# Repricing loads, scans and transposes in the builder of a hybrid encoder kernel, and moving some transfers back in SyncE's order

## The chip, the cores and the metric

The kernel runs on one core of a Trainium2 chip. The metric is the device time of one launch in microseconds (us), lower is better; several runs of a kernel are made and their median is taken. One more execution was recorded by the hardware profiler, and all rows below come from it. The engines are TensorE (PE, with its weight loads as PEld), VectorE (DVE), ScalarE (ACT), GpSimd (POOL) and SyncE (SP), which computes nothing here and issues most of the DMAs. An SPq row is such an issue.

## The reference, cut to what matters

Two layers of a streaming encoder act on 2048 new prompt frames and on 8 running streams of 16 frames, 1024 columns wide. Each layer is one input projection, three mixers beside each other, one output projection and a LayerNorm:

```python
proj = x @ lp["w_in"]
a_sh, a_z, b_q, b_k, b_v, b_f, b_z, c_qkv, c_b, c_a, c_z = split_cols(proj, SPLIT)
o_a, rwkv_last, rwkv_s = rwkv_mix(a_sh, a_z, rwkv_prev, rwkv_s0, lp)
...
o_b = fox_prompt(q, k, v, logf)       # prompt; fox_cached(...) for the streams
...
o_c, conv_last, gdn_s = gdn_mix(c_qkv, c_b, c_a, c_z, gdn_conv_prev, gdn_s0, lp)
h = jnp.concatenate([o_a, o_b, o_c], axis=-1) @ lp["w_out"]
x_new = layer_norm(ALPHA * x + h, lp["ln_g"], lp["ln_b"])
```

`rwkv_mix` and `gdn_mix` are delta-rule recurrences (4 heads of 64 each), which the kernel does in chunks of 64 frames with a small triangular inverse per chunk. `fox_prompt` is causal softmax attention with 8 heads and a cumulative forget term; `fox_cached` is the same against a cache of 1024 rows per stream.

## The kernel before

**Stages.** For each layer the input projection is done in thirds of 640, 768 and 768 columns of tokens (`proj`, line 536). Weights come in blocks of 128 columns (`load_w`, line 427): SyncE loads `wr` (512 KB, two buffers), ACT makes the rounded half `wh`, POOL (or DVE for the v blocks) the rest `wl`. The first time a block is used, `wl` is also stored to the DRAM tensor `wd`; later thirds load it from there. Each product is three matmuls (`pm`, or `pv` for the v blocks). The recurrences (`rwkv_*`, `gdn_*`, `inverse`, `both_chain`, `post`; the "rg" tasks) are woven between the projection's matmuls in sub-blocks of 256 tokens. Then comes attention over the prompt (`fox_prompt`, line 1740), with the streams' attention (`fox_sample`, line 1793) woven in, and at last the output projection (`out_proj`, line 1932).

**What sets the order.** Nothing is measured while the kernel is built. The builder keeps a clock of its own, `Model` (line 105): each instruction gets a start time from when its operands are done, when its output tile is free, and when its engine has room (`place`, line 142), and a cost from `Model.cost` (line 154). The time becomes the instruction's scheduling priority, and for SyncE it also fixes the order: `Eng.order` (line 252) chains each DMA behind the one with the next smaller time, from the recurrences' start to the end of attention in each layer (`pin`). On the chip an engine's queue, SyncE's too, goes in that order and an instruction that waits holds those behind it. TensorE's order comes from the same clock: `Task.wake` and `drive` (line 466) put a task's matmuls between projection matmuls when the clock says that their operands are ready. A wrong price does not change what is waited for on the chip, only who stands in front of whom.

The prices that matter here: a DVE instruction costs 0.065 us plus elements per partition over 960 (1920 for some); a SyncE DMA occupies the queue for max(0.5, bytes / 3.6e5) us and lands 2.0 us later (lines 182 to 186). A read from a DRAM tensor does not wait in the clock for the write to it.

**Places that the change touches.** `load_w` stores `wd`. In `proj` the k and q blocks are split into `khi` and `klo`, which are stored to `ks` and `qs`; their tiles share the tag `z4` (three buffers) with `xin`, the tiles that bring in the tokens of the next third (`load_x`, line 511), and with the log-forget tiles of `logf` (line 677), stored to `ck`, `sm`, `lx` and the outputs. `gate` (line 1512) loads `z` for a recurrence's output. `inverse` and `inverse2` use DVE's square transposes (`N<-NB`, `TT<-Wi`, `T<-TT`); `rwkv_a`, `logf` and `fox_sample` use `tensor_tensor_scan`. `fox_sample` loads cache pieces `kc` and `vc` of 1 MB each, writes its cumulative sums to the DRAM tensor `SC` and reads them back as `S`. `open_o` (line 1918) loads the output weights `wor`, 8 times 512 KB, when `fox_sample` is done. `open_fx` (line 1569) opens attention's tiles once the projection's are free:

```python
self.QA = self.QA0 + [pool.tile([128, 512], F32R, name=f"QA{j}") for j in range(2, 6)]
self.KA = self.KA0 + [pool.tile([128, 1024], F32R, name=f"KA{j}") for j in range(2, 6)]
self.fx_fill(nc.gpsimd, self.KA[2:], self.QA[2:])
self.fx_qa(l, 0, 1)
```

`fx_fill` (line 1550) writes constants into rows 64 and up of these tiles on POOL; `fx_qa` (line 1620) loads rows 0 to 63 of two QA tiles. The attention's first matmuls are `mx` (the row maxima, `fx_max`, line 1634) and `st` (the scores, `fx_exp`, line 1668). Every instruction but a matmul has the helper's line 246 in the profile; matmuls have 224, transposes on TensorE 227.

Of the kernel before, what the change touches and what calls it, by code (L numbers as in the profile page):

```python
# [14 lines left out]
TS = 16  # L15
PAST = 1024
# [88 lines left out]
class Model:  # L105
# [4 lines left out]
    def __init__(self, tc):  # L110
        self.tc, self.t, self.pin = tc, 0.0, 0
        self.done, self.used, self.busy, self.rings, self.by = {}, {}, {}, {}, {}
        self.held = set()

    def tile(self, ap, key, bufs):
# [38 lines left out]
    def cost(self, eng, kind, n, outs, ins):  # L154
        cols = sum(1 for a in ins if numel(a) == 1 and a.shape[0] > 1)
        psum = any(a.space == bass.MemoryType.PSUM for a in ins)
        if eng == "vector":
            fast = kind in ("tensor_scalar", "tensor_copy", "memset") and not psum
            return 0.065 * (1 + cols) + n / (1920.0 if fast else 960.0)
        if eng == "scalar":  # L160
            return (0.05 if psum else 0.095) + 0.09 * cols + n / 1200.0
        if kind == "memset":
            return 0.05 + n / 1220.0
        return 0.05 + 0.27 * cols + n / 440.0

# [100 lines left out]


class NC:
    def __init__(self, nc, model):
        self.tensor = nc.tensor  # L270
        for n in ("vector", "scalar", "gpsimd", "sync"):
            setattr(self, n, Eng(n, getattr(nc, n), model))


# [24 lines left out]
class Trunk:  # L299
# [127 lines left out]
    def load_w(self, pool, key, src, kk, n, eng):  # L427
        nc = self.nc
        raw = pool.tile([128, kk, n], F32, tag="wr", name="wr", bufs=2)
        wh = pool.tile([128, kk, n], F32R, tag="wh", name="wh", bufs=2)  # L430
        wl = pool.tile([128, kk, n], F32R, tag="wl", name="wl", bufs=2)
        for ap, c in src:
            m = ap.shape[1]
            nc.sync.dma_start(raw[:, :, c:c + m], ap.rearrange("(k p) n -> p k n", p=128))
        nc.scalar.copy(wh, raw)
        if key in self.wd:
            nc.sync.dma_start(wl.bitcast(F32), self.wd[key])
        else:
            eng.tensor_tensor(wl, raw, wh.bitcast(F32), op=ALU.subtract)
            self.wd[key] = self.dram.tile([128, kk, n], F32, name="wd_" + "_".join(map(str, key)))  # L440
            nc.sync.dma_start(self.wd[key], wl.bitcast(F32))
        return wh, wl
# [93 lines left out]
    def proj(self, l, ti, groups, nxt=None):  # L536
# [91 lines left out]
        for nm, c0, S, X in (("k", 1664, self.KS[l], self.KX[l]), ("q", 1152, self.QS[l], self.QX[l])):  # L628
            if nm not in groups:
                continue  # L630
            for r in range(0, 512, 128):
# [8 lines left out]
                nc.vector.tensor_tensor(lo[:, ns:n], st[:, ns:n], hi[:, ns:n].bitcast(F32), op=ALU.subtract)  # L640
                nc.sync.dma_start(S[0, r:r + 128, tp], hi[:, ns:n].bitcast(F32))
                nc.sync.dma_start(S[1, r:r + 128, tp], lo[:, ns:n].bitcast(F32))
                if ns:
# [33 lines left out]
    def logf(self, l, ti, fs):  # L677
# [10 lines left out]
        nc.vector.scalar_tensor_tensor(out=lt, in0=f, scalar=0.0, in1=ab, op0=ALU.min, op1=ALU.subtract)  # L688
        nc.sync.dma_start(self.o["fox_logf_p"][l, 0, tp].rearrange("(j p) h -> p j h", p=128), lt[:, ns // 128:])
        if ns:  # L690
            nc.sync.dma_start(self.o["fox_logf_s"][l].rearrange("s t h -> (s t) h"), lt[:, 0])
        nc.vector.tensor_scalar(f, lt, -1.0, None, op0=ALU.mult)
        nc.sync.dma_start(self.SM[l][t0:t0 + n].rearrange("(j p) c -> p j c", p=128), fs[:, :, 8:16])
        yield
# [7 lines left out]
        if ns:  # L702
            nc.sync.dma_start(self.LX[l].rearrange("s h t -> h s t"), fr[0:8, 0:ns].rearrange("h (s t) -> h s t", t=TS))
        cr = pool.tile([8, 768], F32, tag="st", name="cr", bufs=2)
# [5 lines left out]
        self.split(ch[:, ns:n], cl[:, ns:n], cr[:, ns:n], "vector")  # L710
        nc.sync.dma_start(self.CK[l][0, :, tp], ch[:, ns:n].bitcast(F32))
        nc.sync.dma_start(self.CK[l][1, :, tp], cl[:, ns:n].bitcast(F32))

# [577 lines left out]
    def both_chain(self, x):  # L1291
# [66 lines left out]
        if x["t0"] + W == NTOK:  # L1358
            dst = self.o["gdn_wkv_p"][x["l"]].rearrange("s (p h) k v -> s p (h k) v", h=2)
            for p in range(2):  # L1360
                nc.sync.dma_start(dst[0, p], self.Sg[:, p])

# [95 lines left out]
    def gdn_chain(self, x):  # L1458
# [50 lines left out]
        for p in range(2):  # L1509
            nc.sync.dma_start(dst[:, p].rearrange("s k v -> k s v"), SS[:, :, p])  # L1510

    def gate(self, x, r0, y, name):
        nc, W = self.nc, x["W"]
        z = self.rt("z", [128, 2, W])
        nc.sync.dma_start(z, self.PZ[x["l"]][r0:r0 + 256, x["t0"]:x["t0"] + W].rearrange("(q p) t -> p q t", p=128))
# [34 lines left out]
    def fx_fill(self, eng, KA, QA):  # L1550
        for t in QA + KA:
# [17 lines left out]
    def open_fx(self, l):  # L1569
# [223 lines left out]
    def fox_sample(self, l):  # L1793
# [3 lines left out]
        kx = pool.tile([128, 4, 128], F32, name="kx")  # L1797
        nc.sync.dma_start(qx, self.QX[l].rearrange("(c p) t -> p c t", p=128))
        nc.sync.dma_start(kx, self.KX[l].rearrange("(c p) t -> p c t", p=128))
        qbd = pool.tile([128, NS, 4, 32], F32, name="qbd")  # L1800
# [4 lines left out]
        lf = pool.tile([128, NS, 8, 8], F32, tag="vn", name="lf", bufs=2)  # L1805
        nc.sync.dma_start(lf, i["cache_fox_logf"][l].rearrange("s (p j) h -> p s j h", j=8))
        lr = pool.tile([64, PAST + TS], F32, tag="S", name="lr64", bufs=2)
# [5 lines left out]
        def load(s, nm, hf):  # L1813
            if s < NS:
                t = kv[s, nm, hf] = pool.tile([128, 4, 512], F32, tag=nm, name=nm, bufs=4)
                nc.sync.dma_start(t, i["cache_fox_" + nm[0]][l, s, hf * 512:hf * 512 + 512].rearrange("(j p) h d -> p j (h d)", p=128))

# [6 lines left out]
        for j0 in (0, 4):  # L1824
# [3 lines left out]
            nc.scalar.mul(lv[:, j0:j0 + 4], p[0:64].rearrange("p (j t) -> p j t", j=4), -1.0)  # L1828
        nc.sync.dma_start(lr[:, PAST:], self.LX[l].rearrange("s h t -> (s h) t"))
        cr = pool.tile([64, PAST + TS], F32, tag="S", name="cr64", bufs=2)  # L1830
# [78 lines left out]
        z = pool.tile([128, 4, 128], F32, tag="vn", name="sfz", bufs=2)  # L1909
        nc.sync.dma_start(z, self.PZ[l][256:768, 0:SMP].rearrange("(c p) t -> p c t", p=128))  # L1910
# [4 lines left out]
        nc.sync.dma_start(self.OD[l][256:768, 0:SMP].rearrange("(c p) t -> p c t", p=128), oT)  # L1915
        self.close(pool)
# [154 lines left out]
```

## Time and profile before

| | us |
|---|---|
| median of 3 runs | 4135.79 (4131.1 to 4138.03) |
| the profiled execution, its own time | 4139.12 |
| its span in the profile | 4137.2 |
| PE busy, share of the span | 3776.2, 91% |
| DVE, ACT, POOL busy | 2700.3, 1637.1, 1223.7 |
| mean granted TensorE clock | 0.95 |

The span is what the profile covers; the profiled execution's own time lies 1.9 us above it and 3.3 us above the median. PE's busy time counts a matmul as longer when the granted clock is low, so a busy PE is not PE at its peak. Idle time of an engine matters only where PE, the busiest engine, ends up waiting for it. In a timeline row the bracket at the end gives the idle time of the engine before the instruction and what ended it.

### The profile page before, as it was taken

What the parts mean: (1) busy time and instruction counts of PE and PEld (TensorE: products, weight loads), DVE (VectorE), ACT (ScalarE), POOL (GpSimd) and SP (SyncE); (2) the same over time, 40 slices, a digit from 0 to 9 for tenths busy, and PEclk for the clock granted to TensorE, in tenths of its full rate; (3) what the DMA queues carried; (4) which work ended last, traced back from release to release, by engine and by line L of the source; (5) the groups of instructions that cost most, each with busy time, mean ns of one, the idle gap of its engine ahead of it and who ended that gap; (6) DMA issues with size and microseconds to landing.
All of it is one profiled execution on the core that took longest, in us unless ns stands there. A gap on an engine that the chain in (4) does not pass through costs nothing.

```text
span 4137.2 us, 78111 instructions
## 1 busy us (share of the span) xinstructions
PE 3776.2 (91%) x30554; PEld 3107.2 (75%) x30554; DVE 2700.3 (65%) x6029; ACT 1637.1 (40%) x3351; POOL 1223.7 (30%) x1073
## 2 busy tenths in 40 slices
PE   6989998999998799889999898989999888998998
PEld 6988887888887456557888888878888775665577
DVE  6475668677774677774523757577667767777645
ACT  2343434344442344542124434244435424444411
POOL 4311232122212344454222112312122124444522
PEclk9999999999998899999999999999999989999999
DMA  7744545444555677443456445554445555774332
GB/s 262 238 154 129 155 141 173 123 139 127 173 156 138 187 192 195 138 102 111 135 157 192 134 133 151 168 153 127 141 128 186 154 131 164 199 195 124 105 115 102
DMA packets 601754, 633.80 MB, mean 153 GB/s; under 512 B 153625, under 2 KB 457483, under 8 KB 601387
## 3 DMA queue, kind: packets, MB, share of 16 engines
q1 hardware_dynamic: 535228, 543.89, 45.1%
q10 hardware_dynamic: 63406, 76.01, 5.2%
q0 software_dynamic: 2752, 8.92, 0.6%
q8 instruction: 241, 3.95, 0.4%
q14 instruction: 127, 1.03, 0.1%
HBM read 437.59 MB, written 191.10 MB: 152 GB/s over the span
## 4 chain that ended last, share of the span: by engine, by line
PE 54%; DVE 19%; issue 10%; DMA 8%; POOL 4%; ACT 3%; SPq 1%; ACTq 0%; POOLq 0%; DVEq 0%
PE pm L224 21%; PE op L224 6%; PE st L224 5%; PE fo L224 4%; PE mx L224 3%; DVE itmp L246 2%; PE pv L224 2%; DVE Wi L246 2%; PE cr L224 2%; DVE y L246 2%; PE co L224 2%; DMA pc<-pc 2%; DVE xs L246 1%; DVE m L246 1%; PE cg L224 1%
## 5 line engine op out<-in xcount | busy, mean ns | idle before, releaser
L224 PE MATMUL pm<-xh,wh 128*128 128x384 f32 (+1 forms) x2784 | 987.1, 355 | 4.8 <-ACT wh L246 4.8
L224 PE MATMUL pm<-xh,wl 128*128 128x384 f32 (+1 forms) x2784 | 924.5, 332 | 23.4 <-DMA wl<-wd 14.1
L224 PE MATMUL pm<-xl,wh 128*128 128x384 f32 (+1 forms) x2784 | 923.3, 332 | 0.0
L224 PEld LDWEIGHTS pm<-xh,wh 128*128 128x128 f32 x2784 | 533.4, 192 | 43.9 <-issue 17.0
L224 PEld LDWEIGHTS pm<-xh,wl 128*128 128x128 f32 x2784 | 532.6, 191 | 27.1 <-DMA wl<-wd 16.5
L224 PEld LDWEIGHTS pm<-xl,wh 128*128 128x128 f32 x2784 | 534.0, 192 | 10.2 <-issue 9.8
L246 POOL TENSOR_TENSOR acc<-acc,pt 128x512 f32<-128x512 f32 (+2 forms) x336 | 378.3, 1142 | 347.0 <-ACT pt L246 314.0
L246 DVE TENSOR_REDUCE m<-mx 128x1 f32<-128x512 f32 (+3 forms) x640 | 371.4, 605 | 160.4 <-PE mx L224 151.6
L246 ACT ACTIVATE pt<-st 128x512 f32<-128x512 f32 (+3 forms) x640 | 330.9, 533 | 341.8 <-PE st L224 319.7
L246 ACT CAST wh<-wr 128x1024 fp32r<-128x1024 f32 (+1 forms) x198 | 207.3, 1049 | 316.8 <-PE pm L224 237.3
L224 PE MATMUL mx<-KA,QA 66*128 66x512 f32 (+3 forms) x640 | 265.1, 437 | 40.0 <-DMA QA<-qs 26.0
L224 PE MATMUL st<-QB,KB 128*128 128x512 f32 (+3 forms) x640 | 266.7, 417 | 32.1 <-DMA QB<-qs 10.7
L224 PE MATMUL fo<-pt,V 128*64 128x512 f32 (+3 forms) x1280 | 286.8, 570 | 1.1 <-ACT pt L246 1.1
L246 ACT COPY st<-pm 128x384 f32<-128x384 f32 (+1 forms) x348 | 159.2, 457 | 279.7 <-PE pm L224 265.0
L224 PE MATMUL st<-QA,KA 104*128 104x512 f32 (+3 forms) x640 | 244.0, 381 | 0.2
L246 POOL TENSOR_SCALAR SD<-Sr,dl 128x64 f32<-128x64 f32 x128 | 66.9, 537 | 594.5 <-DVE Sr L246 517.9
L224 PEld LDWEIGHTS mx<-KA,QA 66*128 66x128 f32 x640 | 128.8, 206 | 113.3 <-issue 47.0
L224 PE MATMUL op<-woh,oh 128*128 128x512 f32 x544 | 213.0, 392 | 0.7 <-ACT acc L246 0.7
L224 PE MATMUL op<-wol,oh 128*128 128x512 f32 x544 | 212.5, 391 | 0.0
L224 PE MATMUL op<-woh,ol 128*128 128x512 f32 x544 | 212.4, 390 | 0.0
L246 POOL TENSOR_TENSOR wl<-wr,wh 128x1024 fp32r<-128x1024 f32 x58 | 142.1, 2451 | 191.9 <-ACT wh L246 171.6
L246 DVE TENSOR_TENSOR itmp<-N,Wi 128x126 f32<-128x126 f32 (+22 forms) x558 | 178.7, 320 | 15.1
(378 smaller groups left out, 7616.8 us busy)
## 6 DMA issues: line engine op xcount, KB each, us to landing
wr<-in_w_in SPq DMA_DIRECT2D x198, 512.0 KB
wl<-wd SPq DMA_DIRECT2D x116, 512.0 KB
kc<-in_cache_fox_k SPq DMA_DIRECT2D x32, 1024.0 KB
vc<-in_cache_fox_v SPq DMA_DIRECT2D x32, 1024.0 KB
wd<-wl SPq DMA_DIRECT2D x58, 512.0 KB
xin<-xd SPq DMA_DIRECT2D x78, 256.0 KB
y<-xd SPq DMA_DIRECT2D x34, 512.0 KB
ol<-od SPq DMA_DIRECT2D x34, 512.0 KB
```

Source lines behind the costliest of these rows:

```text
L224: self.add(lambda: self.eng.matmul(out, a, b, start=start, stop=stop), out, a, b, cyc, start)
L246: r = f(*a, **b)
```

## The change

The builder's prices: square transposes and scans on DVE cost 0.065 + n/500 (n/960 before); SyncE DMAs occupy the queue at 3.2e5 bytes per us (3.6e5 before) and land 3.0 us later (2.0 before); a read from `SC` waits in the clock for its write. A second handle for SyncE, `nc.lag`, places a DMA 6 us later in the clock than its operands allow. It is the same queue and the same DMA; only its place in the order moves. `open_fx` issues the QA load ahead of the constants and fills two QA tiles ahead of the rest.

```diff
         if eng == "vector":
+            if kind in ("transpose", "tensor_tensor_scan"):
+                return 0.065 + n / 500.0
...
             if a.space == bass.MemoryType.DRAM:
                 dram = True
+                if a.tensor.name.startswith("SC"):
+                    t = max(t, self.done.get(a.tensor.name, 0.0) - self.lag)
...
         if eng == "sync":
             n = max(n * a.shape[0] for a in outs)
-            cost = max(0.5, n * 4 / 3.6e5)
-            end = self.place(eng, t, cost) + 2.0
-            t = end - 2.0 - cost
+            cost = max(0.5, n * 4 / 3.2e5)
+            end = self.place(eng, t + self.lag, cost) + 3.0
+            t = end - 3.0 - cost
...
+class Lag:
+    BY = 6.0
+    def __init__(self, eng, model):
+        self.eng, self.m = eng, model
+    def dma_start(self, *a):
+        self.m.lag = self.BY
+        r = self.eng.dma_start(*a)
+        self.m.lag = 0.0
+        return r
...
-        self.fx_fill(nc.gpsimd, self.KA[2:], self.QA[2:])
         self.fx_qa(l, 0, 1)
+        self.fx_fill(nc.gpsimd, (), self.QA[2:4])
+        self.fx_fill(nc.gpsimd, self.KA[2:], self.QA[4:])
```

These DMAs go from `nc.sync` to `nc.lag`: the stores to `wd` (not those of other tensors in `load_w`), `ks`, `qs`, `ck`, `sm`, `lx`, the log-forget outputs, the `gdn_wkv` outputs of prompt and streams; the loads of `z` in `gate`; and in `fox_sample` the loads of `qx`, `kx`, `lf`, `kc`, `vc`, `lr` and its `z`, and the store of its result to `od`. All loads of `wr`, `wl`, `xin`, `pr`, `pc`, `QA`, `KA`, `QB`, `KB`, `V`, `S` and `wor` stay on `nc.sync`.

## Rows read from the trace of the kernel before

**Rows 1.** The page's first part, PE: busy us, share, instructions.
```profile
PE 3776.2 (91%) x30554; PEld 3107.2 (75%) x30554; DVE 2700.3 (65%) x6029; ACT 1637.1 (40%) x3351; POOL 1223.7 (30%) x1073
```
**Rows 2.** What PE waited for: us in total, times, longest us.
```profile
PE mx L224 <- DMA QA<-qs: 26.0, 6, 11.4
PE pt L227 <- DMA xin<-xd: 24.8, 11, 4.5
...
PE zps L224 <- DVE TT L246: 18.3, 6, 11.0
...
PE st L224 <- DMA QB<-qs: 10.7, 1, 10.7
```
**Rows 3.** PE's timeline at eight waits: start us, us, instruction, idle before.
```profile
76.27 0.42 PE L224 MATMUL pm<-xh,wh 128*128 128x320 f32 x1 [2.91 <-ACT wh L246]
...
1142.26 0.63 PE L227 MATMUL pt<-cst,xin 128*128 128x128 f32 x4 [3.77 <-DMA xin<-xd]
...
1334.16 0.76 PE L224 MATMUL mx<-KA,QA 66*128 66x512 f32 x1 [7.66 <-DMA QA<-qs]
...
1377.35 0.79 PE L224 MATMUL st<-QB,KB 128*128 128x512 f32 x1 [10.66 <-DMA QB<-qs]
...
2705.47 0.66 PE L227 MATMUL pt<-cst,xin 128*128 128x128 f32 x4 [3.51 <-DMA xin<-xd]
...
3223.80 0.31 PE L224 MATMUL zps<-TT,L 32*32 32x32 f32 x2 [11.05 <-DVE TT L246]
...
3371.27 0.53 PE L224 MATMUL mx<-KA,QA 66*128 66x512 f32 x2 [2.16 <-DMA QA<-qs]
...
3830.55 0.77 PE L224 MATMUL mx<-KA,QA 66*128 66x512 f32 x1 [11.42 <-DMA QA<-qs]
```
**Rows 4.** POOL's timeline where the first layer's attention opens (the constants).
```profile
1322.17 1.91 POOL L246 MEMSET QA<- 32x512 f32 x4 [0.68 <-PE sfp L227]
...
1329.58 3.92 POOL L246 MEMSET KA<- 8x1024 f32 x4
```
**Rows 5.** SyncE's queue in the first layer's opening: start of issue, us.
```profile
1321.92 1.09 SPq L246 DMA_DIRECT2D QB<-qs  x2
...
1328.97 1.18 SPq L246 DMA_DIRECT2D QA<-qs  x2
...
1358.16 0.49 SPq L246 DMA_DIRECT2D vc<-in_cache_fox_v  x1
...
1368.67 1.23 SPq L246 DMA_DIRECT2D QB<-qs  x2
```
**Rows 6.** Stretches after long waits: start:end, length, busy us of each engine, clock.
```profile
1342.00:1373.00 31.00, 18.18 (x75) 12.81 (x73) 18.53 (x41) 9.31 (x16) 7.05 (x8) 0.61 0.81 214
1379.00:1397.00 18.00, 17.31 (x66) 9.92 (x66) 15.25 (x24) 8.23 (x15) 9.48 (x8) 0.81 0.54 130
3226.00:3244.00 18.00, 18.00 (x205) 16.63 (x201) 10.98 (x23) 10.41 (x21) 1.25 (x3) 0.82 0.26 79
3833.00:3855.00 22.00, 20.94 (x85) 12.13 (x87) 14.32 (x29) 9.13 (x18) 6.30 (x6) 0.77 0.71 179
```
**Rows 7.** Groups by line, DVE's transposes and scan: busy us, mean ns.
```profile
L246 DVE STREAM_TRANSPOSE TT<-Wi 32x512 f32<-32x512 f32 x72 | 79.6, 1106 | 1.8
L246 DVE STREAM_TRANSPOSE N<-NB 128x1024 f32<-128x1024 f32 x18 | 36.5, 2030 | 0.4
L246 DVE TENSOR_TENSOR_SCAN cs<-reset,sw 128x256 f32<-128x256 f32 (+1 forms) x36 | 22.5, 650 | 3.5 <-ACT sw L246 3.4
```
**Rows 8.** SyncE's queue early in layer 0.
```profile
76.23 0.29 SPq L246 DMA_DIRECT2D ck<-ch  x1
```
**Rows 9.** SyncE's queue late in the second layer's attention.
```profile
3812.89 9.62 SPq L246 DMA_DIRECT2D wor<-in_w_out  x8
```
**Rows 10.** The chain of waits: start us, us from issue to landing.
```profile
181.23 5.57 DMA pc<-pc
...
466.97 2.99 DMA z<-pz
```

More of the change, by code (lines that the diff above doesn't have):

```diff
@@ L113, in __init__ @@
         self.held = set()
+        self.lag = 0.0
     def tile(self, ap, key, bufs):
@@ L272, in __init__ @@
             setattr(self, n, Eng(n, getattr(nc, n), model))
+        self.lag = Lag(self.sync, model)
 class Pool:
@@ L440, in load_w @@
             self.wd[key] = self.dram.tile([128, kk, n], F32, name="wd_" + "_".join(map(str, key)))
-            nc.sync.dma_start(self.wd[key], wl.bitcast(F32))
+            nc.lag.dma_start(self.wd[key], wl.bitcast(F32))
         return wh, wl
@@ L640, in proj @@
                 nc.vector.tensor_tensor(lo[:, ns:n], st[:, ns:n], hi[:, ns:n].bitcast(F32), op=ALU.subtract)
-                nc.sync.dma_start(S[0, r:r + 128, tp], hi[:, ns:n].bitcast(F32))
-                nc.sync.dma_start(S[1, r:r + 128, tp], lo[:, ns:n].bitcast(F32))
+                nc.lag.dma_start(S[0, r:r + 128, tp], hi[:, ns:n].bitcast(F32))
+                nc.lag.dma_start(S[1, r:r + 128, tp], lo[:, ns:n].bitcast(F32))
                 if ns:
@@ L688, in logf @@
         nc.vector.scalar_tensor_tensor(out=lt, in0=f, scalar=0.0, in1=ab, op0=ALU.min, op1=ALU.subtract)
-        nc.sync.dma_start(self.o["fox_logf_p"][l, 0, tp].rearrange("(j p) h -> p j h", p=128), lt[:, ns // 128:])
+        nc.lag.dma_start(self.o["fox_logf_p"][l, 0, tp].rearrange("(j p) h -> p j h", p=128), lt[:, ns // 128:])
         if ns:
-            nc.sync.dma_start(self.o["fox_logf_s"][l].rearrange("s t h -> (s t) h"), lt[:, 0])
+            nc.lag.dma_start(self.o["fox_logf_s"][l].rearrange("s t h -> (s t) h"), lt[:, 0])
         nc.vector.tensor_scalar(f, lt, -1.0, None, op0=ALU.mult)
-        nc.sync.dma_start(self.SM[l][t0:t0 + n].rearrange("(j p) c -> p j c", p=128), fs[:, :, 8:16])
+        nc.lag.dma_start(self.SM[l][t0:t0 + n].rearrange("(j p) c -> p j c", p=128), fs[:, :, 8:16])
         yield
@@ L702, in logf @@
         if ns:
-            nc.sync.dma_start(self.LX[l].rearrange("s h t -> h s t"), fr[0:8, 0:ns].rearrange("h (s t) -> h s t", t=TS))
+            nc.lag.dma_start(self.LX[l].rearrange("s h t -> h s t"), fr[0:8, 0:ns].rearrange("h (s t) -> h s t", t=TS))
         cr = pool.tile([8, 768], F32, tag="st", name="cr", bufs=2)
@@ L710, in logf @@
         self.split(ch[:, ns:n], cl[:, ns:n], cr[:, ns:n], "vector")
-        nc.sync.dma_start(self.CK[l][0, :, tp], ch[:, ns:n].bitcast(F32))
-        nc.sync.dma_start(self.CK[l][1, :, tp], cl[:, ns:n].bitcast(F32))
+        nc.lag.dma_start(self.CK[l][0, :, tp], ch[:, ns:n].bitcast(F32))
+        nc.lag.dma_start(self.CK[l][1, :, tp], cl[:, ns:n].bitcast(F32))
     def open_rg(self, l):
@@ L1360, in both_chain @@
             for p in range(2):
-                nc.sync.dma_start(dst[0, p], self.Sg[:, p])
+                nc.lag.dma_start(dst[0, p], self.Sg[:, p])
     def rwkv_chain(self, x):
@@ L1509, in gdn_chain @@
         for p in range(2):
-            nc.sync.dma_start(dst[:, p].rearrange("s k v -> k s v"), SS[:, :, p])
+            nc.lag.dma_start(dst[:, p].rearrange("s k v -> k s v"), SS[:, :, p])
     def gate(self, x, r0, y, name):
@@ L1514, in gate @@
         z = self.rt("z", [128, 2, W])
-        nc.sync.dma_start(z, self.PZ[x["l"]][r0:r0 + 256, x["t0"]:x["t0"] + W].rearrange("(q p) t -> p q t", p=128))
+        nc.lag.dma_start(z, self.PZ[x["l"]][r0:r0 + 256, x["t0"]:x["t0"] + W].rearrange("(q p) t -> p q t", p=128))
         nc.gpsimd.tensor_tensor(y, y, z, op=ALU.mult)
@@ L1550, in fx_fill @@
     def fx_fill(self, eng, KA, QA):
-        for t in QA + KA:
+        for t in (*QA, *KA):
             eng.memset(t[64:96].bitcast(F32), 0.0)
@@ L1797, in fox_sample @@
         kx = pool.tile([128, 4, 128], F32, name="kx")
-        nc.sync.dma_start(qx, self.QX[l].rearrange("(c p) t -> p c t", p=128))
-        nc.sync.dma_start(kx, self.KX[l].rearrange("(c p) t -> p c t", p=128))
+        nc.lag.dma_start(qx, self.QX[l].rearrange("(c p) t -> p c t", p=128))
+        nc.lag.dma_start(kx, self.KX[l].rearrange("(c p) t -> p c t", p=128))
         qbd = pool.tile([128, NS, 4, 32], F32, name="qbd")
@@ L1805, in fox_sample @@
         lf = pool.tile([128, NS, 8, 8], F32, tag="vn", name="lf", bufs=2)
-        nc.sync.dma_start(lf, i["cache_fox_logf"][l].rearrange("s (p j) h -> p s j h", j=8))
+        nc.lag.dma_start(lf, i["cache_fox_logf"][l].rearrange("s (p j) h -> p s j h", j=8))
         lr = pool.tile([64, PAST + TS], F32, tag="S", name="lr64", bufs=2)
@@ L1815, in load @@
                 t = kv[s, nm, hf] = pool.tile([128, 4, 512], F32, tag=nm, name=nm, bufs=4)
-                nc.sync.dma_start(t, i["cache_fox_" + nm[0]][l, s, hf * 512:hf * 512 + 512].rearrange("(j p) h d -> p j (h d)", p=128))
+                nc.lag.dma_start(t, i["cache_fox_" + nm[0]][l, s, hf * 512:hf * 512 + 512].rearrange("(j p) h d -> p j (h d)", p=128))
         pieces = [(nm, hf) for nm in ("kc", "vc") for hf in range(2)]
@@ L1828, in fox_sample @@
             nc.scalar.mul(lv[:, j0:j0 + 4], p[0:64].rearrange("p (j t) -> p j t", j=4), -1.0)
-        nc.sync.dma_start(lr[:, PAST:], self.LX[l].rearrange("s h t -> (s h) t"))
+        nc.lag.dma_start(lr[:, PAST:], self.LX[l].rearrange("s h t -> (s h) t"))
         cr = pool.tile([64, PAST + TS], F32, tag="S", name="cr64", bufs=2)
@@ L1909, in fox_sample @@
         z = pool.tile([128, 4, 128], F32, tag="vn", name="sfz", bufs=2)
-        nc.sync.dma_start(z, self.PZ[l][256:768, 0:SMP].rearrange("(c p) t -> p c t", p=128))
+        nc.lag.dma_start(z, self.PZ[l][256:768, 0:SMP].rearrange("(c p) t -> p c t", p=128))
         g = pool.tile([128, 4, 128], F32, tag="vn", name="sfg", bufs=2)
@@ L1914, in fox_sample @@
         nc.vector.tensor_tensor(oT, oT, g, op=ALU.mult)
-        nc.sync.dma_start(self.OD[l][256:768, 0:SMP].rearrange("(c p) t -> p c t", p=128), oT)
+        nc.lag.dma_start(self.OD[l][256:768, 0:SMP].rearrange("(c p) t -> p c t", p=128), oT)
         self.close(pool)
```

## The prediction, made before the changed kernel was seen

> **What bounds the kernel now.** I read the page first: PE is busy 91% of the span [rows 1], so the time is PE's work plus PE's waits. The change adds and removes no arithmetic, so it can only alter waits, and the clock that PE is granted after them. So the second view is what PE waited for. Those four lines [rows 2] are what this change can reach: 26.0 us for QA loads, 24.8 for `xin`, 18.3 for the DVE tile `TT`, 10.7 for one QB load, 79.8 in all, 1.9% of the span. Third, PE's timeline, for where these waits are and how long each is [rows 3]: most of the sum lies in a few waits of 7 to 11 us. Fourth, the queues of POOL and SyncE in those places [rows 4, 5, 8, 9], for who stood ahead of the late instruction. Last, the stretches behind the long waits [rows 6]: the granted clock is 0.61 to 0.82 there, a mixture of full speed and the lower of the two levels, so a wait costs more than itself. What the clock costs I take as PE's busy time there times one minus the clock: 18.18 x 0.39 = 7.1 us behind the waits of the first opening, 17.31 x 0.19 = 3.3 behind the QB wait, 18.00 x 0.18 = 3.2 behind the wait for `TT`, 20.94 x 0.23 = 4.8 behind the wait at 3830.55.
>
> **The change, part by part.** All gains and losses are against the profiled execution of 4139.1 us.
>
> *Opening of attention.* In the first layer PE waits 7.66 us at 1334.16 for a QA load [rows 3]. The builder's clock put that load behind the constants, since it takes both for writes of one tile; so SyncE issued it at 1328.97, 7.05 us after the first QB load at 1321.92 [rows 5], though POOL's constants [rows 4] do not gate it: it went out before they ended at 1329.58 + 3.92 = 1333.50. Written first, it gets the earliest place. Its landing is then like that of a load of twice the size, 2.99 us [rows 10], so about 1325, with PE ready for it at 1334.16 - 7.66 = 1326.5. The constants of the two tiles that PE needs now come first on POOL: four of the eight QA writes, about 1.9 us [rows 4]. They too are done in time. The same wait in the second layer, 2.16 us, goes as well. What moves back is six or so QB, KB and V loads, by one issue of 1.18 us [rows 5]; PE reads them only after some 10 us of `mx` work. So -9.8, and at most half of the 7.1 us of clock, because other short waits in that stretch stay: -3. I take -13; bounds 0 and -17.
>
> *QB at 1377.35.* The load was issued at 1368.67 and PE went on 8.7 us later [rows 3, 5]; pieces of the streams' cache, 1 MB each, had gone out just before (1358.16) and DMA was busy 0.81 of the stretch [rows 6]. With `nc.lag` the cache pieces stand 6 us later, so one or two come behind QB. I take 6 of the 10.66 us and 2 of the 3.3 us of clock: -8; bounds 0 and -14.
>
> *Transposes and scans.* The old prices are 0.065 + 1024/960 = 1.13 us for `N<-NB` and 0.60 for `TT<-Wi`; the trace has 2.03 and 1.11; a scan of 256 had 0.33, the trace 0.65 [rows 7]. New: 2.11, 1.09, 0.58. Per sub-block DVE was booked short by 0.9 + 4 x 0.5 + 2 x 0.3 = 3.5 us, so PE's matmuls on `TT` were ordered too early by about that. Nothing hides it: those matmuls block the projection's behind them. Two waits, 11.05 [rows 3] and one of a shorter kind, hold most of the 18.3 us [rows 2]. Each can lose at most 3.5; I take -5 and -2 of the clock, -7; bounds 0 and -21 (all of it and 3.2).
>
> *Stores of the log-forget terms, early.* At 76.27 PE waits 2.91 us for `wh`, whose weight load stood behind those stores and `wd` in SyncE's queue; at 76.23 SyncE was held until DVE had made `ch` [rows 3, 8]. The stores now stand 6 us later. -3; bounds 0 and -5 (about twice the wait that is seen, since the next block is late too). The later `wd` store holds its `wl` buffer up to 6 us longer; there are two buffers and a block is 48 matmuls of some 0.15 us, 7 us, so the store is done within the next block. Price 0; if DMA is full, up to +5.
>
> *Stores of k and q.* Here the change adds waiting. `xin` needs a `z4` buffer that `khi` or `klo` gives back only when its store has landed. At 1142.26 and 2705.47 PE already waits 3.77 and 3.51 us on that path [rows 3], so nothing covers a further delay. There are four such crossings, two in each layer. The store goes later only as far as a load that the clock now puts ahead of it has to wait for its own buffer, 0 to 6 us; I take 1.5 each, the low end, since most loads in such a window find theirs free: +6; bounds 0 and +24.
>
> *`z` in `gate`, results, `SC`.* The recurrence's output has a whole sub-block before the next needs its tile, so 6 us on `z` are covered by that; in the opening, where `fox_sample` waits for two such gates, up to 12 us are covered by the more than 100 us between its end and the output projection. `S` behind `SC`: SyncE no longer stands waiting for a write with loads behind it; PE had no wait there. Price 0; bounds +4 and -4.
>
> *w_out.* At 3812.89 eight loads of 512 KB go out at once, and a QA load behind them lets PE wait 11.42 us at 3830.55 [rows 3, 9]. No edit is meant for this. But `S` after `SC`, the lag and the longer landing push `fox_sample` back in the clock by 10 us or more, and the eight loads with it, by when QA's place is ahead of them. Ends 0 and -16 (11.42 + 4.8), or a new one in the first layer, +11; I take half, -8.
>
> *Landing.* Between a 256 KB load that took 2.99 us and a 512 KB load that took 5.57 [rows 10] lie both prices: the old clock has 2.73 and 3.46 for these sizes, the new one 3.82 and 4.64. For a queue with nothing ahead the old one is right, for a full one the new one. What comes late in the clock gets its consumers ordered later on ACT, DVE and TensorE, which takes away short waits (`xin`, 24.8 us [rows 2]) where loads are slow and costs nothing where PE has other matmuls. I take 0; bounds +6 and -10. The page "DMA: Bandwidth & Descriptors" of the Trainium skill, in "Anatomy of one DMA — SWDGE (gpsimd) path", speaks against the change: its fit, for DMAs issued from GpSimd, is a fixed 2.0 us plus bytes over 436 thousand per us, which makes an estimate of 3.2 us for 512 KB, below even the old price; this case's 5.57 us disagrees. By that page the new landing would be an overcharge of 1.4 us per load and this part would give nothing.
>
> *The new order itself.* Times of all tasks shift, so all short waits are dealt anew. What an order that nobody has looked at costs I bound by the waits of its own kind: two more like 3.77, or one like 11.05 [rows 3], at worst three; I take +10; bounds 0 and +30.
>
> **The sum.** -13 - 8 - 7 - 3 + 6 - 8 + 10 = -23. The profiled execution would be 4116; the median stands 3.3 us below it, so 4112.5 us; I say 4112.
>
> **The rivals.** *Nothing much (same).* The order changes less than its prices: SyncE mostly waits for buffers, so it issues the same loads at the same moments. For it: a large part of the queue's idle time is waiting for PE. Against it: the opening's wait hangs on a place that is rewritten, not repriced. It would give the opening alone, 9.8, against +6 from the k and q stores: about 4132. To this belongs the overcharge on landing told above.
>
> *Slower.* The place is `z4` in the projection. A store that stands 6 us later is put behind a `wl` or `pr` load whose buffer is not free; SyncE holds there, `xin` comes a full 6 us late at each of four crossings, +24, and the token transposes stand in PE's order with nothing in front to fill. With the opening's gain -13 and the order's +10 this gives +21: about 4157. It decides from the point where the added delay at a crossing exceeds some 4 us. For it: two of the crossings wait already. Against it: the chip does not wait for a place in time, only for what stands ahead, and the lag orders most stores behind loads that are free to go.
>
> *More.* The big waits go whole: opening 17, QB 14, w_out 16, `TT` 14, with nothing new: -61, about 4075.
>
> **How the numbers follow.** A measurement of this kernel can tell about 0.2% from no change, 8 us. Forecast (4095 to 4127): 0.50. More: 0.13. Nothing much (4128 to 4144): 0.16. Slower: 0.21, with 4157 as its middle. So faster 0.63, same 0.16, slower 0.21. The range 4084 to 4150 leaves out the far part of "more" and the upper half of "slower", about 0.18 together; the likeliest case alone has 4095 to 4127.
>
> **What would show it.** Right: in the first layer's opening SyncE issues the two QA loads first and PE's wait of 7.66 us is gone; the cache pieces stand behind QB and KB loads; PE's total for `TT` falls to some 12 us; no QA load behind eight w_out loads; mean clock above 0.95. Wrong: PE's waits for `xin` rise from 24.8 towards 45; or SyncE's queue shows loads standing behind a lagged transfer's neighbour; or the opening's wait is replaced by one for QB, KB or POOL's constants, which would show that the DMA engines and not the place were the limit there.

## The result, and the profile after

The changed kernel took 4161.3 us (median of 4 runs, 4153.7 to 4166.4) beside 4135.8 for the kernel before on the same chip: a ratio of 1.0056, 95% interval 1.0038 to 1.0074. It is slower by some 23 us, where I had said 4112. The profiled execution took 4166.4 us, its span is 4164.6, 27.4 longer than before.

PE's row on the page answers to [rows 1]:

```profile
PE 3796.3 (91%) x30554; PEld 3114.5 (75%) x30554; DVE 2703.2 (65%) x6029; ACT 1630.2 (39%) x3351; POOL 1219.2 (29%) x1073
```

PE was busy 20.1 us longer with the same instructions, and its idle time (span less busy) rose only from 361.0 to 368.3. So three quarters of the loss is no wait at all: the same matmuls ran slower. The trace's clock records show where: they have two levels, full speed and half, and PE was busy 323.5 us at the lower one before and 363.0 us now. Half of that is what the lower level costs, 161.8 and 181.5 us. Without it PE's work, counted at full speed, is 3614 us in both kernels. The mean granted clock is 0.948 (0.950 before), where I had asked for above 0.95.

What PE waited for (us in total, times, longest us) answers to [rows 2]:

```profile
PE st L229 <- DVE m L251: 38.5, 34, 2.9
...
PE pm L229 <- DMA wl<-wd: 30.5, 10, 5.0
...
PE zps L229 <- DVE TT L251: 16.8, 8, 4.6
PE lp L229 <- DVE acc L251: 15.7, 2, 7.9
PE pt L232 <- DMA xin<-xd: 14.9, 7, 2.9
...
PE mx L229 <- DMA QA<-qs: 3.5, 3, 1.6
```

The waits that I aimed at shrank: QA from 26.0 to 3.5, `xin` from 24.8 to 14.9, `TT` from 18.3 to 16.8 with its longest from 11.0 to 4.6, and the QB wait of 10.7 to 0.9. Others took their place: `st` for the row maxima `m` 6.9 before, `wl` from `wd` 14.1, `lp` 5.7. The opening itself went as the prediction's last part asks. SyncE's queue there (start, us of issue), against [rows 5]:

```profile
1275.13 1.11 SPq L251 DMA_DIRECT2D QA<-qs  x2
1276.29 1.24 SPq L251 DMA_DIRECT2D QB<-qs  x2
```

and PE's first wait of over 1 us in that opening, against 7.66 us in [rows 3] (a small part came back as a wait for POOL's constants):

```profile
1282.29 0.90 PE L229 MATMUL mx<-KA,QA 66*128 66x512 f32 x2 [1.14 <-POOL QA L251]
```

**Where the time went.** Four rows of PE's timeline tell it: the last projection matmul `pm` of the first layer, the last matmul `vp` of the recurrences, the last `sft` of the streams' attention, and the first `op` of the output projection. Before:

```profile
1321.73 0.31 PE L224 MATMUL pm<-xh,wl 128*128 128x320 f32 x1
...
1334.73 1.91 PE L224 MATMUL vp<-O,cst 128*128 128x512 f32 x2
...
1727.52 0.27 PE L227 MATMUL sft<-cst,os 128*128 128x128 f32 x1
...
1897.65 0.76 PE L224 MATMUL op<-woh,oh 128*128 128x512 f32 x1 [0.69 <-ACT acc L246]
```

After:

```profile
1274.79 0.31 PE L229 MATMUL pm<-xh,wl 128*128 128x320 f32 x1
...
1453.52 1.02 PE L229 MATMUL vp<-O,cst 128*128 128x512 f32 x2
...
1871.83 0.27 PE L232 MATMUL sft<-cst,os 128*128 128x128 f32 x1
...
1910.52 0.79 PE L229 MATMUL op<-woh,oh 128*128 128x512 f32 x1 [1.62 <-ACT oh L251]
```

The recurrences now end 179.4 us behind the projection's last matmul (14.6 before; in the second layer 180.3, and 56.7 before). I call this the **tail**. The projection is shorter by 46.9 us, mostly since this work has left it; attention, from there to the first `op`, is longer by 59.8 (635.4 against 575.6). The second layer has the same picture, -43.4 and +56.3. Work that only moves costs nothing: counted at full speed, about 36 and 26 us of PE's work went from projection to attention. What attention has on top is 13 and 9 us from the lower clock and 12 and 21 us of idle time; the projection gives back 13 us of idle time in each layer. In the code the streams' attention hangs on the recurrences' last task (`tail`, which first closes their buffers). So its loads start behind the tail too: in the first layer the first `kc` piece went out at 1348.15 before, 26 us into attention, and now at 1469.44, 194 us into it. It ends 38 us ahead of the output projection where there were 170.

The windows show the tail. Columns are start:end, length, busy us (and number) of PE, PEld, DVE, ACT and POOL, granted clock, DMA share, GB/s; the stretches are the first 180 us of the first layer's attention and the rest of it. Before:

```profile
1322.00:1502.00 180.00, 145.75 (x849) 91.42 (x846) 121.44 (x230) 69.82 (x127) 77.08 (x74) 0.86 0.68 184
1502.00:1897.00 395.00, 363.96 (x2227) 217.28 (x2225) 281.56 (x499) 189.01 (x356) 192.52 (x163) 0.94 0.52 139
```

After:

```profile
1275.00:1455.00 180.00, 148.18 (x1159) 91.91 (x1159) 130.12 (x306) 57.36 (x118) 69.54 (x73) 0.78 0.28 65
1455.00:1910.00 455.00, 409.74 (x2682) 248.31 (x2680) 329.02 (x576) 217.72 (x411) 218.44 (x186) 0.96 0.59 167
```

In the tail the granted clock is 0.78 in the mean of the stretch (0.86 before), a mixture of its two levels; behind it the clock is higher than before, 0.96 against 0.94. DMA has little to do in the tail, and afterwards 455 us remain instead of 395.

DVE is not full in the tail (130 of 180 us), yet the row maxima stand behind the recurrences' pieces in its order. Its timeline ahead of a wait of 2.30 us by `st` (start, us, operation):

```profile
1317.08 0.60 DVE L251 TENSOR_TENSOR NB<-eqp,DM 32x128 f32<-32x128 f32 x2
1317.70 0.42 DVE L251 TENSOR_TENSOR Eq<-eqp,DM 128x256 f32<-128x256 f32 x1
1318.15 0.59 DVE L251 TENSOR_TENSOR L<-eqp,g 32x128 f32<-32x128 f32 x2
1318.78 0.29 DVE L251 TENSOR_REDUCE m<-mx 128x1 f32<-128x128 f32 x1
```

```profile
1319.12 0.69 PE L229 MATMUL st<-QB,KB 128*128 128x384 f32 x1 [2.30 <-DVE m L251]
```

Not every tail brings this wait: the changed kernel without the lag, below, has a tail of 165 us and waits 11.6 us for `m` in all, where the changed kernel waits 38.5.

### The profile page after: what moved, and what is told of

The parts are those of the page before. It is cut to its first block, busy times and chain, and to the rows that moved or that the text cites. A ratio compares the mean times of both kernels' runs of the same rounds, so it can differ in the third digit from the quotient of the medians.

```text
span 4164.6 us, 78040 instructions
## 1 busy us (share of the span) xinstructions
PE 3796.3 (91%) x30554; PEld 3114.5 (75%) x30554; DVE 2703.2 (65%) x6029; ACT 1630.2 (39%) x3351; POOL 1219.2 (29%) x1073
## 5 line engine op out<-in xcount | busy, mean ns | idle before, releaser
L229 PE MATMUL pm<-xh,wl 128*128 128x384 f32 (+1 forms) x2784 | 930.0, 334 | 44.6 <-DMA wl<-wd 30.5
L229 PE MATMUL st<-QB,KB 128*128 128x512 f32 (+3 forms) x640 | 275.9, 431 | 42.0 <-DVE m L251 38.5
L229 PE MATMUL fo<-pt,V 128*64 128x512 f32 (+3 forms) x1280 | 301.6, 595 | 4.6 <-ACT pt L251 4.6
L229 PEld LDWEIGHTS st<-QB,KB 128*128 128x128 f32 x640 | 126.8, 198 | 98.8 <-DVE m L251 52.4
```

The costliest lines, as they stand in the source:

```text
L229: self.add(lambda: self.eng.matmul(out, a, b, start=start, stop=stop), out, a, b, cyc, start)
```

## The experiments

Theory A, formed on the traces above: dearer prices make the recurrences' steps ready later in the builder's clock, they fall out of the projection, and the tail in attention costs more than the projection gains ("spill theory" or "tail theory" in the expectations). Rival B: one part does harm of its own (rivals 1 and 2 for the lag and for landing; "theory L" is B for landing). Rival C: each new order deals its waits by chance, and nothing systematic is there. "Rows behind" in the expectations counts the recurrences' matmul rows behind the last `pm` in TensorE's program order.

### Each part alone

```diff
# one_fill: QA load ahead of the constants
-        self.fx_fill(nc.gpsimd, self.KA[2:], self.QA[2:])
         self.fx_qa(l, 0, 1)
+        self.fx_fill(nc.gpsimd, (), self.QA[2:4])
+        self.fx_fill(nc.gpsimd, self.KA[2:], self.QA[4:])
# one_lag: the transfers called with nc.lag, 6 us
-            end = self.place(eng, t, cost) + 2.0
+            end = self.place(eng, t + self.lag, cost) + 2.0
# one_land
-            cost = max(0.5, n * 4 / 3.6e5)
-            end = self.place(eng, t, cost) + 2.0
+            cost = max(0.5, n * 4 / 3.2e5)
+            end = self.place(eng, t, cost) + 3.0
# one_dve
+            if kind in ("transpose", "tensor_tensor_scan"):
+                return 0.065 + n / 500.0
```

**QA order.** Expected:

> The kernel before with the QA load ahead of the constants alone. All theories: the waits of 7.66 and 2.16 us at attention's opening go, the rest stays nearly in place (5 and 133 rows): -10 to 0 us. If it does not get faster, the DMA engines and not the place held that load.

Measured: 4113.6 us, ratio 0.9945 (0.9928 to 0.9963); more than expected.

**Lag.** Expected:

> The kernel before with the lag of 6 us alone, without prices, the SC rule and the QA order. Spill theory: 61 rows behind the last projection matmul in both layers, more than before in the first and fewer in the second: -8 to +5 us. Rival 1: +15 to +30 us, with waits for xin or wl above those of before. Rival 2: within 5 us.

Measured: 4137.1 us, 1.0002 (0.9989 to 1.0015); as A and rival 2 have it.

**Landing.** Expected:

> The kernel before with SyncE's new rate and landing alone. Spill theory: 133 rows behind the last projection matmul in both layers, so the first layer gets like the second: 0 to +8 us. Rival 1: within 5 us. Rival 2: +15 to +30 us, with PE's waits for wl going from 14 towards the 30 us of the changed kernel.

Measured: 4182.7 us, 1.0105 (1.0080 to 1.0131); above every expectation. Rival 2's sign is there: PE's waits for `wl`, from `wd` and `wd_v`, are 26.8 us (14.6 before).

**DVE prices.** Expected:

> The kernel before with the new DVE prices alone (square transposes, scans). Theory, the spill: the dearer DVE steps make the builder place the recurrences' matmuls later among the projection's, so that more of them fall behind the last projection matmul (in TensorE's order 229 rows in each layer, against 5 and 133 before and 382 after) into attention, where DVE's row maxima hold PE. It expects +8 to +25 us, PE's waits st<-DVE m well above 6.9 us, and a clock near 0.8 in the first 160 us of attention. Rival 1, the lagged transfers cost it: no change here, within 5 us. Rival 2, the longer landing of loads costs it: no change here, within 5 us.

Measured: 4143.2 us, 1.0015 (1.0004 to 1.0026); just below A's range. A's signs are there: the wait for `m` is 18.6 us, and the clock 0.81 in the first 160 us of attention.

What follows: the QA order is a gain of some 23 us (0.55% of 4136), landing a loss of 43, the DVE prices of 6, the lag nothing. What PE waited for in the kernel with the lag alone:

```profile
PE mx L225 <- DMA QA<-qs: 47.2, 6, 13.0
PE zps L225 <- DVE TT L247: 40.1, 12, 8.2
```

Its QB wait is gone (0.4 us), and the waits for QA and `TT` have grown by 43 us together, yet its idle time in all is 357.0 us (361.0 before): other waits went in exchange. With the QA order alone the QB wait is gone too, so the two terms that I had for the opening's QA and QB waits were not independent.

### The change without one part

```diff
# less_fill, less_lag, less_land, less_dve: the reverse of the part above, in the changed kernel; for the lag
-    BY = 6.0
+    BY = 0.0
```

**Without the QA order.** Expected:

> The changed kernel with the QA load behind the constants again. If the gain of the QA order (one_fill, 0.9945) holds in the new order too: 4175 to 4195, ratio 1.009 to 1.014, with PE's waits for QA at attention's opening back. If it was due to the old order: 4155 to 4170.

Measured: 4173.4 us, 1.0068 (1.0053 to 1.0083); between the two expectations.

**Without landing.** Expected:

> The changed kernel with SyncE's old rate and landing (3.6e5, 2.0). Theory L, the longer landing is what costs (one_land, ratio 1.0105) and the parts nearly add up: about 42 us below the changed kernel's 4161, 4115 to 4130, ratio to the kernel before 0.995 to 0.999. Spill theory (recurrences behind the last projection matmul, here 469 rows against 382): no faster than the changed kernel, 4155 to 4185, ratio 1.005 to 1.012.

Measured: 4140.3 us, 0.9997 (0.9985 to 1.0009); against A; 24 us below the changed kernel, where theory L has 42.

**Without the DVE prices.** Expected:

> The changed kernel with DVE's old prices. Theory L with parts that add: 4150 to 4162, ratio 1.003 to 1.006. Spill theory (141 rows against 382): 4125 to 4145, ratio 0.998 to 1.002. If the dearer transposes heal what the longer landing spoils (PE's waits for TT were 36.9 us with landing alone, 16.8 in the changed kernel): above 4170, ratio over 1.008.

Measured: 4135.3 us, 0.9984 (0.9968 to 1.0000); as A has it.

**Without the lag.** Expected:

> The changed kernel with the lag at 0 in place of 6 us (the order rule for S behind SC stays): 374 and 374 rows behind the projection, 382 with it. Tail theory: the tail is the same, so within 20 us of the changed kernel, 4141 to 4181. If the lag did the harm by late stores of k and q (the rival that the prediction called slower): 4137 or less, with the waits for xin under 10 us.

Measured: 4197.5 us, 1.0153 (1.0123 to 1.0183); outside both expectations, on the far side.

What follows: beside the others (1.0056 less these ratios, of 4136 us) the QA order is worth -5 us (not clear of noise), the lag -40, landing +24, the DVE prices +30. Alone they were -23, 0, +43, +6. No part has a price of its own. The lag, worth nothing alone, is here the best part of the change; without it PE waits as follows, 31.0 us for `wd_v` (2.7 with the lag) and 20.3 for QA (3.5):

```profile
PE pv L229 <- DMA wl<-wd_v: 31.0, 6, 6.5
...
PE mx L229 <- DMA QA<-qs: 20.3, 3, 9.9
...
PE pt L232 <- DMA xin<-xd: 14.9, 9, 3.2
```

The `xin` row is the same with and without the lag: late stores of k and q, the rival that I had called "slower", do not show as a cost.

### The tail by itself

`drive` lets a recurrence take its next step only when `mix` times the last step's length has passed in the clock. `mix` is no part of the change and touches no price; a smaller one packs the recurrences closer into the projection.

```diff
# base_mix08, base_mix09, spill_up (1.3): the kernel before; after_mix08, mix05 (0.5): the changed one
-            self.pe.keep, self.mix, self.ring = True, 1.0, ((f"psR{l}", "gr"), 2)
+            self.pe.keep, self.mix, self.ring = True, 0.8, ((f"psR{l}", "gr"), 2)
```

**Changed kernel, 0.8.** Expected:

> The changed kernel with the recurrences given a larger share of the projection (mix 0.8 instead of 1.0), which alters no price: 141 rows instead of 382 stand behind the last projection matmul. Spill theory: 4120 to 4145, ratio 0.996 to 1.002. Theory L: the landing is still in every place of the order, 4150 to 4170, ratio 1.003 to 1.008.

Measured: 4117.0 us, 0.9938 (0.9921 to 0.9954), 44 us below the changed kernel and just below A's range, with attention at 580 and 591 us.

**Changed kernel, 0.5.** Expected:

> The whole changed kernel with the share at 0.5: 53 and 53 rows behind the projection, the fewest that this number gets with all prices in (0.8 left 141 and gave 4117). Spill theory: attention 550 to 570 us, the time 4085 to 4110. If the earlier recurrences hold up the projection instead, the projection grows by as much: 4117 or more.

Measured: 4091.9 us, 0.9886 (0.9870 to 0.9902), attention 559 and 560 us: as A has it.

**Kernel before, 1.3.** Expected:

> The kernel before with the recurrence's share raised from 1.0 to 1.3 and nothing else: 326 and 326 of its rows stand behind the projection's last matmul in TensorE's order, where the kernel before has 5 and 133 and the changed kernel 382 and 382. Spill theory: attention takes 615 to 640 us in each layer (changed kernel 635 and 638, before 576 and 582), the projection wins back half of it, and the time is 4150 to 4175. Luck of the order: 4136 give or take 20, with attention's own time unmoved.

Measured: 4188.8 us, 1.0126 (1.0105 to 1.0147), attention 651 and 659 us. A's direction, and more than its upper end. With no price altered, this order has tails of 157 and 166 us and takes 52 us longer; PE's waits for QA are 48.2 us in it (26.0 before), so the 52 us are not the tail's alone.

**Kernel before, 0.8.** Expected:

> The kernel before with one number altered: the share of its own time that the recurrence is given beside the projection, 1.0 to 0.8 (more of it is put early). No price and no order rule of the change is in it. In TensorE's program order 0 and 0 rows of the recurrence then stand behind the projection's last matmul (layer 0, layer 1), where the kernel before has 5 and 133. Spill theory (the changed kernel lost its time because 382 rows in each layer were pushed behind the projection): there is nearly nothing to pull back here, so -15 to +5 us, 4121 to 4141. Rival (0.8 is simply a better number, and the 44 us that it gave in the changed kernel have nothing to do with the spill): about -40, 4090 to 4100.

Measured: 4066.7 us, 0.9823 (0.9808 to 0.9839). That is the rival's side, and better than both expectations. The count of rows had misled me: 5 and 133 rows are few, but the tails were 14.6 and 56.7 us long, and they went to nothing, with attention at 545 and 542 us in place of 576 and 582. That the tail made the 70 us is not shown: PE's busy time at the lower clock level fell from 323.5 to 218.9 us, and 35 of these 105 us lie in the projection.

**Kernel before, 0.9.** Expected:

> The kernel before with the share at 0.9: again 0 and 0 rows behind the projection, but another order than with 0.8. Tail theory: attention 545 to 560 us in each layer and the time 4065 to 4095. Luck: attention has no reason to stay at 545, and the time lies between 4067 (0.8) and 4136 (1.0) or outside both, most likely about 4100 to 4130.

Measured: 4106.2 us, 0.9932 (0.9907 to 0.9958). Attention is 557 and 554 us as A said, but the time is 11 us above A's range and 40 above the kernel with 0.8, which has no tail either. So it lies where C expected it, and these 40 us are not the tail's; which step of the order makes them stays open.

The first 180 us of the first layer's attention with 0.8 in the kernel before, no tail, columns as above:

```profile
1310.00:1490.00 180.00, 151.02 (x917) 96.48 (x915) 132.23 (x248) 71.83 (x136) 80.93 (x79) 0.88 0.75 201
```

and with 1.3, tail 157 us:

```profile
1263.60:1443.60 180.00, 141.55 (x1072) 86.91 (x1073) 136.11 (x303) 63.53 (x125) 77.58 (x79) 0.82 0.34 83
```

### Without a tail, with parts of the change

```diff
# fill_mix08: QA order and 0.8; land_nospill: landing and 0.8; noland_nospill: the change less landing, and 0.8
-            self.pe.keep, self.mix, self.ring = True, 1.0, ((f"psR{l}", "gr"), 2)
+            self.pe.keep, self.mix, self.ring = True, 0.8, ((f"psR{l}", "gr"), 2)
```

**QA order.** Expected:

> The kernel before with the QA load ahead of its constants, and the share 0.8 in place of 1.0. 0 and 0 rows behind the projection. The QA order alone gave 4113.6. Spill theory: little more than that, 4100 to 4115. Rival (0.8 gives 40 us wherever it is): about 4075. If the early recurrences cost the projection more than the attention wins, 4118 or more.

Measured: 4078.4 us, 0.9854 (0.9838 to 0.9869). That is the rival's number (0.8 is worth its 40 us and more wherever it is), not A's. The gain of 23 us does not come on top of the 70 from 0.8; another QA load is late now, with PE waiting 13.4 and 12.7 us for it.

**Landing.** Expected:

> The kernel before with the whole landing price, which alone gave +42 us, and the share 0.8: 0 and 0 rows behind the projection. Spill theory: attention falls to some 545 us per layer, as in the kernel before with 0.8 (545 and 542), and the time is 4070 to 4100. If landing's harm is its own (loads and the matmuls on TT ordered badly inside the projection, where that run waited 36.9 us for TT): 4066 + 42, 4105 or more, with the waits for TT still over 30 us and attention at 545.

Measured: 4165.7 us, 1.0065 (1.0049 to 1.0081). Here B has it: with no tail the kernel is still 99 us above the one without the price. Attention is 13 and 24 us longer, but the projection is 39 and 27 longer. Not through `TT`, as I had written (8.7 us). These of its waits grew (from 15.3, 15.5, 10.2 and 7.3 us without the price):

```profile
PE mx L225 <- DMA QA<-qs: 46.0, 8, 15.7
...
PE pv L225 <- DMA wl<-wd_v: 23.7, 5, 9.1
PE pv L225 <- ACT wh L247: 21.1, 6, 6.7
PE pm L225 <- ACT wh L247: 20.8, 7, 6.5
```

**The change less landing.** Expected:

> The changed kernel without its landing price and with the share 0.8: 1 and 1 rows behind the projection. QA order, lag, DVE prices and S behind SC are in. Spill theory: attention about 545 us, the time 4060 to 4090, and it was 4140 with 469 rows. Luck of the order: 4140 less the 44 that 0.8 gave in the changed kernel, 4096, or anything about it, with no tie to attention.

Measured: 4106.4 us, 0.9920 (0.9905 to 0.9936), 16 us above A's upper end, with attention at 557 and 554 and not at 545; C's side.

### Landing's halves

```diff
# land_latency
-            end = self.place(eng, t, cost) + 2.0
+            end = self.place(eng, t, cost) + 3.0
# land_rate
-            cost = max(0.5, n * 4 / 3.6e5)
+            cost = max(0.5, n * 4 / 3.2e5)
```

**The fixed part.** Expected:

> The kernel before with one half of the landing price: 3.0 us in place of 2.0 behind every SyncE transfer, the rate left at 3.6e5. Rows behind the projection 229 and 229. The whole landing price alone gave +42 us. If the fixed landing does the harm (loads ordered later, so the recurrence's inputs and with them its matmuls later): +25 to +45, 4160 to 4180, with the waits for TT that came with the whole price. If the rate does it: within 8 us of the kernel before. If it is the luck of each order rather than either price: anything, and the two halves do not add up to 42.

Measured: 4121.4 us, 0.9946 (0.9927 to 0.9966): a gain, against every expectation but the last.

**The rate.** Expected:

> The kernel before with the other half: 3.2e5 in place of 3.6e5 (a 1 MB load is 0.36 us dearer, a 256 KB load 0.09), the landing left at 2.0. Rows behind the projection 61 and 61. By size alone this is a tenth to a third of the other half, so within 8 us of the kernel before, 4128 to 4144. If the luck of each order decides: as far away as the other half, some 10 to 40 us either way.

Measured: 4139.8 us, 1.0002 (0.9990 to 1.0015).

Halves of -22 and 0 make a whole of +43. So landing's harm is not in either price by itself but in the order that both together give, and which step of that order does it stays open.

### All kernels by tail

Read from PE's timeline of each kernel as above: tail, then length of the projection (with the start) and of attention, first | second layer, us.

| kernel | tail | projection | attention | median |
|---|---|---|---|---|
| before, 0.9 | none | 1317, 1287 | 557, 554 | 4106 |
| before, 0.8 | none | 1310, 1279 | 545, 542 | 4067 |
| QA order, 0.8 | none | 1319, 1278 | 551, 548 | 4078 |
| landing, 0.8 | none | 1349, 1306 | 559, 566 | 4166 |
| change less landing, 0.8 | 5, 5 | 1327, 1286 | 557, 554 | 4106 |
| QA order | 13, 54 | 1321, 1273 | 554, 578 | 4114 |
| before | 15, 57 | 1322, 1274 | 576, 582 | 4136 |
| change, 0.5 | 28, 27 | 1320, 1270 | 559, 560 | 4092 |
| rate | 34, 34 | 1322, 1289 | 569, 573 | 4140 |
| lag | 35, 35 | 1324, 1271 | 572, 577 | 4137 |
| change, 0.8 | 59, 59 | 1305, 1266 | 580, 591 | 4117 |
| change less DVE prices | 60, 60 | 1309, 1274 | 584, 581 | 4135 |
| landing | 60, 67 | 1328, 1295 | 588, 591 | 4183 |
| fixed part | 100, 100 | 1311, 1264 | 590, 585 | 4121 |
| DVE prices | 122, 120 | 1296, 1256 | 603, 600 | 4143 |
| before, 1.3 | 157, 166 | 1264, 1226 | 651, 659 | 4189 |
| change less lag | 165, 166 | 1294, 1254 | 629, 631 | 4198 |
| change less landing | 169, 169 | 1264, 1216 | 646, 642 | 4140 |
| change | 179, 180 | 1275, 1231 | 635, 638 | 4161 |
| change less QA order | 182, 188 | 1271, 1230 | 637, 648 | 4173 |

A straight line through each layer's twenty pairs (no tail taken as 0): attention grows 0.5 us per us of tail (correlation 0.97 in both layers), the projection shrinks 0.3 (-0.88), and what is left is 0.19 per us. About this line the sum of both scatters by 12 and 14 us per layer, and its correlation with the tail is 0.73 and 0.66.

So the tail tells attention's length well and the kernel's time badly. The four kernels with no tail at all lie between 4067 and 4166, and the four with tails of 165 to 188 us between 4140 and 4198. The fixed part and the DVE prices, with tails of 100 and 120 us, are 22 us faster and 6 slower than the kernel before, where the line gives 24 and 32 slower. Of the 14 times that A named, 3 came true (the lag, the change less DVE prices, the change with 0.5); 5 kernels were faster than A's range and 6 slower.

## Why the prediction was wrong

**The step that failed** is "the new order itself", +10 with bounds 0 and +30. I bounded it by waits of PE of the kind that the trace of before showed, and I took the clock only as something that mended waits give back. Three quarters of the loss is not idle time, so no such bound could hold it: 19.7 of the 27.4 us are the price of the lower clock level (181.5 less 161.8). It falls in attention, where the recurrences' work now stands and pays 13 and 9 us more for that level in its two layers. Idle time adds 7.3.

How much of this the tail made stays open. By the line, a tail longer by 164.8 and 123.6 us is worth 0.19 x 288 = 55 us, an estimate; `mix` alone, with no price touched, moved the kernel before by 122 us between 0.8 and 1.3, but kernels without any tail are 99 us apart too. With 55 in place of 10 my sum of -23 becomes +22, and 23 was measured. That this fits is luck: the single terms are further off, landing above all, and the line misses single kernels by up to 57 us.

**Transposes and scans**, -7, bounds 0 and -21. The mechanism is right: with this part alone PE has no wait for `TT` left, and the change without it waits 35.4 us. In the changed kernel the longest such wait fell from 11.0 to 4.6, but the total only from 18.3 to 16.8, where I had asked for some 12. I had booked a dearer price as mended waits alone; it also makes every step of a recurrence ready later, and so makes a tail: 122 us long with this part alone, 15 before. The part cost 6 us alone and 30 in company.

**Landing**, 0, bounds +6 and -10. Measured +43 alone and +24 in company, far outside: the second term that failed. I had weighed whether the price was right and not what the order does with it. Whether 3.0 is nearer to the chip than 2.0 decided nothing: half of the price alone was a gain.

**Opening**, -13, bounds 0 and -17. The mechanism is right, place and load as told; alone it gave 23, and 21 of that is in the first layer's attention (554.2 for 575.6). It took the QB wait with it, which I had given to the lag as a term of -8. Beside the rest it was worth 5, not clear of noise.

**Stores of k and q**, +6. The `xin` wait fell by 9.9 us, with the lag and without it, so nothing was added there, and the slower rival's place was wrong though its side was right. PE's wait for `wl` from `wd` rose from 14.1 to 30.5 us, but the late store, priced at 0 with +5 at most, is not shown to have caused it: with the lag alone that wait is 8.4 us, and without the lag it is 9.1 while the one for `wd_v` is 31.0 (2.7 with it).

**Log-forget stores**, -3: the wait at 76.27 is 1.33 us now, about half. **w_out**, -8: no QA load waits behind `wor` any more; but the streams' attention now ends 38 us ahead of the output projection, so the output weights come only then, and DVE splits them (`wol`) in front of the sums `acc` that PE needs:

```profile
1890.25 8.96 DVE L251 TENSOR_TENSOR wol<-wor,woh 128x1024 fp32r<-128x1024 f32 x4
...
1900.34 5.61 DVE L251 TENSOR_TENSOR wol<-wor,woh 128x1024 fp32r<-128x1024 f32 x3
...
1906.82 2.08 PE L229 MATMUL lp<-acc,ones 128*64 128x512 f32 x4 [7.82 <-DVE acc L251]
```

In the second layer the same wait is 7.89 us; both together were 5.7 before. I had called the delay of `z` covered by "more than 100 us" there. That cover is what the tail used up.

**The page's fit for landing.** By the fit in the Trainium skill (page "DMA: Bandwidth & Descriptors", section "Anatomy of one DMA — SWDGE (gpsimd) path"), the prediction reckoned that the landing part would give nothing. That fit is for DMAs issued from GpSimd, and no run here measures it. The part gave +43 alone, and half of its price alone was a gain; so what it did went through the order, and not by how well the price fits.

`S` behind `SC` was not tried by itself: the kernel with the lag alone lacks it, the one without the lag has it.

Of the rivals, "slower" gave 4157, 4 us from the median, by a mechanism that did not happen; that is luck. "Nothing much", 4128 to 4144, falls 17 us short.

## What to carry to other kernels

When a builder's prices set the order, a price is not only a wait mended or missed: it moves work across a stage's border. Such a move can cost clock without any wait, so a bound taken from waits is no bound. Read where the woven work ends against the stage that covers it, in us and not in instructions, before booking any wait: that gave attention's length here, though not the kernel's time. The number that says how densely work is woven, 0.8 in place of 1.0, was worth 70 us (4066.7 us, ratio 0.9823, faster than both kernels), and with almost no tail the change's better prices showed no gain over it (4092 and 4106 against 4067 and 4106).

## What the runs showed of the hardware

The granted clock did not follow PE's busy share: in the first 180 us of attention it was 0.78 with PE busy 148.18 us (the changed kernel) and 0.88 with 151.02 us (the kernel before with 0.8). A busy share counts a matmul at the lower level as longer; counted at full speed, PE's work in these two stretches is 114 and 138 us. What else differs in the rows is the kind of work, 1159 matmuls against 917, and DMA, 0.28 against 0.75. Which of these goes with the clock was not tried.

In the 20 kernels PE's busy time at the lower level in attention grows by 0.22 and 0.27 us per us of tail in the two layers (correlation 0.86 and 0.78), and its idle time there by 0.14. Counted at full speed PE's work is nearly the same in all of them, 3606 to 3623 us, while its busy time runs from 3721 to 3806.
